# Seven products instead of eight for the last input quarter of an MLP product, and weight sums made between DRAM tensors

## The chip, the cores and the metric

The kernel runs on one core of one Trainium2 chip. The metric is the device time of one execution in microseconds, given as the median of several runs; smaller is better. A core has TensorE (PE, matrix products into the PSUM memory), VectorE (DVE), ScalarE (ACT) and GpSimd (POOL) for element-wise work, SyncE (SP), which here only issues transfers, and DMA engines that move data between DRAM and the on-chip memory. Each engine works through its own list of instructions in order and waits for the others by semaphores.

## The reference

One decoder layer on 512 tokens of width 1024, all in float32: a gated linear attention and a dilated attention, merged by gates, then an MLP, then a gated side input and a norm. The change concerns the MLP:

```
h2 = rmsnorm(x, ln2[i])
x = x + jnp.square(jax.nn.relu(h2 @ w_mlp1[i])) @ w_mlp2[i]
h3 = rmsnorm(x, ln3[i])
x = x + jax.nn.sigmoid(h3 @ w_pg[i]) * (p[i] @ w_pp[i])
return rmsnorm(x, ln_f)
```

`w_mlp1` is 1024 x 4096 and `w_mlp2` 4096 x 1024. The hidden vector of 4096 is the input of the second product; its four quarters of 1024 are summed up one after the other.

## The kernel before, in words

**Three products for one.** TensorE takes float32 operands in a rounded form (`F32R`). To keep float32 precision each operand is split into a high half `hi` (a rounded copy, made by ScalarE, line 324 for weights and 474 for activations) and a low half `lo` (the difference, made by VectorE, line 302), and a product becomes hi x hi, hi x lo and lo x hi (helpers `three`, `strassen`, `wide`; all of them issue their matmuls in `run`, line 338).

**Seven products for eight.** Most large products are cut into 2 x 2 blocks and computed with seven block products in the manner of Strassen and Winograd. The weight side needs the blocks A11, A12, A22 and the sums S1 = A21 + A22, S2 = S1 + A11, S4 = S2 + A12 and S3 = A11 + A21 (signs are absorbed elsewhere); the activation side needs B11, B21, B22 and the sums T1 to T4. For the first MLP product (`w_mlp1`) there are eight products `m1q0` to `m1q7`, each a call of `strassen` with seven stages of 24 matmuls of 256 columns. For the second (`w_mlp2`) `m2_seven` goes through the list `MLP2` of pairs (operand, quarter): each pair is one step of 24 matmuls of 512 columns, fed by two weight tiles of 128 x 1024. Before the change `SEVEN = (1, 2, 3)`: quarter 0 is computed plainly by `m2_plain(0)` and `m2_plain(1)`, two times 96 matmuls of 512 columns with eight weight tiles, ahead of `m2_seven`.

**Weights.** All weight tiles are lined up in `OPERANDS`. `weight(name)` calls `fetch`, which works ahead of TensorE: for tile i it issues the low half on VectorE, for i + 1 the high half on ScalarE, for i + 2 sums (`sums`), for i + 3 the load (`prepare`, `load`: an SP transfer of 512 KB, line 245). Here i is two tiles ahead of the one that TensorE is to use. There are eight raw buffers (`NRAW`), five for high halves and four for low halves (`NW = 5`, `NW - 1`). A sum is made in one of two ways. Either POOL issues a transfer that adds the second block onto the first while it lands (`accum_op`; line 253 for the sums listed in `EARLY`, line 281 for S3 of the 256-column products, line 319 for S4 behind the low half of S2), or VectorE adds two tiles (lines 266, 269, 275, 278, 284).

**Side work.** `run` issues matmuls in pieces, and after each piece `step` takes one closure from the list `later` and, every `pace` columns, one step from the generators in `side`. So the order of the element-wise work on each engine is fixed by hand, between the matmuls. `hid_operands` is such a generator: for each pair of `MLP2` it makes the differences T1 to T4 on VectorE (lines 1538 and 622), the high halves on ScalarE and the low halves on VectorE, two tiles of 128 x 512 each. Activations live in one pool of 68 tiles (`NU`).

**The two ends.** At the start TensorE runs `NWARM` matmuls on a tile of ones (line 566) until the first operands are there; the first product (line 594) needs `xh`, made by ScalarE from x, and `hi`, made by ScalarE from the weights (line 579). At the end the last row block of the last product (`pg1`) is cut at column `LAST = 384` into two pieces; each goes through a gate on ScalarE (line 1710), two VectorE steps (lines 1716, 1717) and a square on ScalarE (line 1721), and the root (line 1736) and the output wait for the second piece. `final` finishes a block of the second MLP product: it adds onto the residual x (line 1575, in `onto`), squares it for the norm (line 1603), and transposes it on TensorE (line 1608).

Of the kernel before, what the change touches and what calls it, by code (L numbers as in the profile page):

```python
# [19 lines left out]
P = 128  # L20
# [14 lines left out]
def att_col(g, which):  # L35
# [6 lines left out]
MLP2 = (("A11", 1), ("S1", 1), ("S2", 1), ("A11", 2), ("S1", 2), ("S4", 1), ("S2", 2), ("A11", 3), ("S1", 3), ("S4", 2),  # L42
        ("S2", 3), ("A12", 1), ("S4", 3), ("A12", 2), ("S3", 1), ("S3", 2), ("S3", 3), ("A12", 3),
        ("A22", 1), ("A22", 2), ("A22", 3))
XOF = {"A11": "B11", "S1": "T1", "S2": "T2", "S4": "B22", "A12": "B21", "S3": "T3", "A22": "T4"}
SEVEN = (1, 2, 3)


def weight_units():
# [44 lines left out]
    for sub in range(2):  # L94
        tm(f"m2p{sub}", "w_mlp2", sub * 512)
# [58 lines left out]
def early():  # L154
    after_wide = False
    for n, i in OPERAND.items():
        q, _, what = n.partition(".")
        if what == "S1":
            EARLY.setdefault(max(i - (4 if after_wide else 6), 0), []).append((n, f"{q}.A21", f"{q}.A22"))
            after_wide = False  # L160
        elif what[:3] == "S1." and q.startswith("m2c"):
# [21 lines left out]
LAST = 384  # L183
# [3 lines left out]
NWARM = 9  # L187
# [3 lines left out]
def block_kernel(ctx, tc, xT, x, ws, pT, wts, wha, wa2, vec, lnf, rel, onehot, ident_d, mask_d, out):  # L191
# [51 lines left out]
    def load(name):  # L243
        w = wst.tile([P, 1024], F32, tag="w", name="w")
        SY.dma_start(w, wts[UNIT[name]])
        return w

    def prepare(i):

        name = OPERANDS[i]  # L250
        for n, a, b in EARLY.get(i, ()):
            w = raw[n] = load(a)
            GP.dma_start(w, wts[UNIT[b]], accum_op=OP.add)  # L253
        if name in UNIT:
            raw[name] = load(name)
        elif name in S4_LOADED:
            raw[name] = load(name.replace("S4", "A12"))

    S4_LOADED = [f"m2c{SEVEN[-1]}.S4.{i}" for i in range(2)]

    def sums(i):
        q, _, what = OPERANDS[i].partition(".")
        if q.startswith("m2c"):
            if what[:3] == "S2.":
                w = raw[OPERANDS[i]] = raw[f"{q}.S1{what[2:]}"]
                V.tensor_tensor(w, w, raw[f"{q}.A11{what[2:]}"], op=OP.add)
            elif OPERANDS[i] in S4_LOADED:
                w = raw[OPERANDS[i]]
                V.tensor_tensor(w, w, raw[f"{q}.S2{what[2:]}"], op=OP.add)
        elif q == "wo" and what[:3] == "S4.":  # L270
# [35 lines left out]
    def fetch(upto):  # L306

        while done[0] < min(upto, len(OPERANDS) - 1):
            i = done[0] = done[0] + 1
            if i >= 0:  # L310
# [6 lines left out]
                if (q == "wo" or q.startswith("m2c")) and what[:3] == "S2." and f"{q}.S4{what[2:]}" not in S4_LOADED:  # L317
                    w = raw[f"{q}.S4{what[2:]}"] = raw[OPERANDS[i]]
                    GP.dma_start(w, wts[UNIT[f"{q}.A12{what[2:]}"]], accum_op=OP.add)
# [255 lines left out]
    for k in range(KC):  # L575
# [3 lines left out]
        S.activation(hi, wr[k], AF.Copy)  # L579
# [658 lines left out]
    def gates(name, i, res, make):  # L1238
# [8 lines left out]
        strassen(f"{name}{i}", xs_op, finish)  # L1247
# [35 lines left out]
    later.extend(merge(j) for j in range(KC))  # L1283
    for i in range(2):
        gates("ga", i, ga, sigmoid)
# [207 lines left out]
    hid, hb, hx = [None] * 8, {}, {}  # L1493
# [4 lines left out]
    def quad(q):  # L1498


        def finish(m, t, s, ps):
# [5 lines left out]
            def act():  # L1507
                if q // 2 in SEVEN:
                    S.activation(s, s, AF.Square)  # L1509
                    hb[q, m, t] = s  # L1510
                    return
                for n in range(2):
                    j = 4 * q + 2 * n + m
                    if hid[j] is None:
                        hid[j] = u32()
                    S.activation(hid[j][:, halves(t)], s[:, halves(n)], AF.Square)
# [3 lines left out]
        strassen(f"m1q{q}", x1_op, finish, extra=first_splits(0) if q == 7 else None)  # L1520

    hs = {}

    def hid_splits(n):
        for k in range(len(hs), len(hs) + n):
            hs[k] = split(hid[k])

    def first_splits(n):

        def extra(i):  # L1530
            if 3 <= i:
                later.append(lambda: hid_splits(1))
        return extra

    def hid_operands():
# [5 lines left out]
        for op, c in MLP2:  # L1541
            name = XOF[op]
            b11, b12, b21, b22 = ([hb[2 * c + g, k, t] for g in range(2)] for k in range(2) for t in range(2))
# [24 lines left out]
    drain()  # L1568
# [3 lines left out]
    def onto(m, t, n, ps, neg=None):  # L1572

        o, c = x2[m, t, n], 2 * t + n
        V.scalar_tensor_tensor(out=o, in0=ps, scalar=norm2[m if neg is None else neg][:, c:c + 1], in1=o, op0=OP.mult, op1=OP.add)

    def m2_plain(sub):

        ps = [mmt() if sub else smt() for _ in range(4)]
        for kk in range(4):  # L1580
            wh, wl = weight(f"m2p{sub}.{kk}")
            mms = []
            for k in range(2 * kk, 2 * kk + 2):
                xh, xl = hs[k]
                for tt in range(4):
                    c, w = slice(tt * P, (tt + 1) * P), slice((k % 2) * 512, (k % 2 + 1) * 512)
                    mms += [(ps[tt], xh[:, c], wh[:, w], k == 0, False), (ps[tt], xl[:, c], wh[:, w], False, False),
                            (ps[tt], xh[:, c], wl[:, w], False, k == 7)]
            run(mms)
            if len(hs) < 8:  # L1590
                hid_splits(2)
                if len(hs) == 8:
                    side.append(hid_operands())
        for tt in range(4):
            later.append(lambda tt=tt: onto(sub, tt // 2, tt % 2, ps[tt], 0))

    def final(m, t, n, ps, bank):
# [17 lines left out]
        later.append(go)  # L1615
        later.append(lambda: later.append(turn))
# [244 lines left out]
```

## Time and profile before

| | |
|---|---|
| median of three runs | 947.93 us (946.8 to 948.13) |
| the profiled execution | 946.6 us, its span 944.8 us |
| granted TensorE clock, mean | 0.998 |
| first MLP product, from the chain | 569.93 to 731.22 us |
| plain quarter of the second, from the chain | 731.22 to 774.78 us |
| packets of DMA | 158.75 MB, 168 GB/s over the span |

The profile shows one execution. The span is the time from the first to the last instruction; the execution's own time is a little longer. The chain is the work that ended last, followed back from the end: at each step to what released it, or to the instruction before it on its engine. Rows of it give the start, the length, the engine and the line, and how many instructions were merged. Groups give an instruction's line, engine, operation, output and inputs, shape and count, then busy time and mean ns, then the idle time of the engine ahead of it. Matmuls overlap in the pipeline, so their mean duration is longer than their spacing.

### The profile page before, as it was taken

How to read it: one execution, taken by the hardware profiler on the slowest of the kernel's cores; microseconds unless marked ns; L12 is line 12 of the kernel's file. 1: busy time of each engine (PE TensorE's matmuls, PEld its weight loads, DVE VectorE, ACT ScalarE, POOL GpSimd, SP SyncE). 2: the span in 40 equal slices, each digit the busy share in tenths (PEclk: the TensorE clock that was granted, in tenths of full speed). 3: DMA queues.
4: the chain of work that ended last, by engine and by line, in shares of the span. 5: the costliest groups of instructions: out<-in, count | busy, mean ns of one | idle time of the engine just before them, and what ended most of it. 6: DMA issues, size and time to landing. Idle time of an engine off the chain costs nothing.

```text
span 944.8 us, 15151 instructions
## 1 busy us (share of the span) xinstructions
PE 936.2 (99%) x5860; PEld 844.8 (89%) x5860; DVE 737.9 (78%) x1040; ACT 555.6 (59%) x918; POOL 113.2 (12%) x157
## 2 busy tenths in 40 slices
PE   9999999999999999999999999999999999999996
PEld 8789998899988888999988889999999888888886
DVE  7698869866789579978968779776677789897664
ACT  7357546545675578775743578665556536655543
POOL 0150010120100012022100300100000101021000
PEclk9999999999999999999999999999999999999999
DMA  9474482873817456555654788666546718599202
GB/s 356 141 234 113 133 202 68 280 237 109 189 58 212 166 134 201 135 134 179 183 148 116 177 216 256 161 172 179 157 112 166 191 49 194 148 268 368 88 1 90
DMA packets 49354, 158.75 MB, mean 168 GB/s; under 512 B 7108, under 2 KB 7696, under 8 KB 49281
## 3 DMA queue, kind: packets, MB, share of 16 engines
q1 hardware_dynamic: 31104, 103.76, 31.6%
q0 software_dynamic: 14496, 49.51, 26.5%
q10 hardware_dynamic: 3680, 4.51, 1.3%
q8 instruction: 46, 0.75, 0.3%
q14 instruction: 28, 0.22, 0.1%
HBM read 149.32 MB, written 10.26 MB: 169 GB/s over the span
## 4 chain that ended last, share of the span: by engine, by line
PE 96%; issue 1%; DVE 1%; DMA 1%; ACT 0%; POOL 0%; POOLq 0%; DVEq 0%; ACTq 0%
PE mmt L338 75%; PE smt L338 12%; PE mmt L594 2%; PE smt L1028 2%; DMA u<-y_dram 1%; PE smt L968 1%; PE smt L891 1%; PE smt L566 0%; PE smt L861 0%; PE smt L985 0%; PE smt L984 0%; PE smt L860 0%; PE smt L974 0%; PE smt L1412 0%; PE smt L1084 0%
## 5 line engine op out<-in xcount | busy, mean ns | idle before, releaser
L338 PE MATMUL mmt<-ur,hi 128*128 128x256 f32 (+1 forms) x2192 | 436.4, 297 | 0.0
L338 PEld LDWEIGHTS mmt<-ur,hi 128*128 128x128 f32 x2192 | 349.7, 189 | 11.8
L302 DVE TENSOR_TENSOR lo<-w,hi 128x1024 fp32r<-128x1024 f32 x254 | 308.6, 1219 | 60.5 <-PE mmt L338 37.0
L338 PE MATMUL mmt<-ur,lo 128*128 128x256 f32 (+1 forms) x1096 | 326.6, 298 | 0.5 <-DVE lo L302 0.5
L324 ACT ACTIVATE hi<-w 128x1024 fp32r<-128x1024 f32 x254 | 265.4, 1055 | 101.9 <-PE mmt L338 24.8
L338 PE MATMUL mmt<-hi,ur 128*128 128x512 f32 (+3 forms) x912 | 266.2, 375 | 0.0
L338 PEld LDWEIGHTS mmt<-ur,lo 128*128 128x128 f32 x1096 | 206.6, 189 | 6.3 <-DVE lo L302 0.7
L338 PEld LDWEIGHTS mmt<-hi,ur 128*128 128x128 f32 x912 | 165.3, 188 | 28.6
L338 PE MATMUL mmt<-lo,ur 128*128 128x512 f32 (+3 forms) x456 | 170.6, 374 | 0.0
L474 ACT ACTIVATE ur<-u 128x512 fp32r<-128x512 f32 x113 | 67.5, 625 | 65.3 <-DVE u L622 17.1
L338 PEld LDWEIGHTS mmt<-lo,ur 128*128 128x128 f32 x456 | 85.7, 188 | 15.1
L338 PE MATMUL smt<-hi,ur 128*128 128x512 f32 x288 | 89.1, 390 | 0.0
L302 DVE TENSOR_TENSOR ur<-u,ur 128x512 fp32r<-128x512 f32 x112 | 73.6, 685 | 10.8 <-ACT ur L474 10.2
L467 DVE TENSOR_TENSOR u<-u,mmt 128x512 f32<-128x512 f32 (+1 forms) x94 | 58.0, 648 | 27.2 <-PE mmt L338 26.9
L253 POOL DMA_DIRECT2D w<-in_wts_dram x46 | 43.5, 993 | 249.8 <-DMA w<-in_wts_dram 145.3
L408 ACT ACTIVATE u<-mmt 128x512 f32<-128x512 f32 x72 | 42.9, 596 | 51.0 <-PE mmt L338 50.8
L338 PEld LDWEIGHTS smt<-hi,ur 128*128 128x128 f32 x288 | 53.8, 188 | 10.9
L338 PE MATMUL smt<-lo,ur 128*128 128x512 f32 x144 | 56.0, 389 | 0.0
L281 POOL DMA_DIRECT2D w<-in_wts_dram x18 | 16.1, 894 | 282.0 <-DVE w L278 158.1
L338 PEld LDWEIGHTS smt<-lo,ur 128*128 128x128 f32 x144 | 27.0, 188 | 5.7
L1509 ACT ACTIVATE u<-u 128x512 f32<-128x512 f32 x24 | 15.0, 628 | 26.7 <-DVE u L1505 26.7
L844 ACT ACTIVATE u<-u,st 128x256 f32<-128x256 f32 (+1 forms) x32 | 15.6, 488 | 12.5 <-DVE st L840 11.0
(242 smaller groups left out, 848.0 us busy)
## 6 DMA issues: line engine op xcount, KB each, us to landing
w<-in_wts_dram SPq DMA_DIRECT2D x182, 512.0 KB, 5.1
w<-in_wts_dram POOLq DMA_DIRECT2D x70, 512.0 KB, 7.1
u<-in_xT_dram SPq DMA_DIRECT2D x8, 256.0 KB, 5.2
u<-in_ws_dram SPq DMA_DIRECT2D x8, 256.0 KB, 5.3
v_dram<-u ACTq DMA_DIRECT2D x8, 256.0 KB, 6.4
u<-v_dram POOLq DMA_DIRECT2D x8, 256.0 KB, 6.5
y_dram<-u ACTq DMA_DIRECT2D x8, 256.0 KB, 2.2
u<-y_dram POOLq DMA_DIRECT2D x8, 256.0 KB, 7.0
```

The lines of the kernel that those rows point to most:

```text
L253: GP.dma_start(w, wts[UNIT[b]], accum_op=OP.add)
L281: GP.dma_start(w, wts[UNIT[f"{q}.A21"]], accum_op=OP.add)
L302: V.tensor_tensor(lo, x, hi.bitcast(F32), op=OP.subtract)
L324: S.activation(hi[:, s], w[:, s], AF.Copy, scale=1.0 if c is None else c)
L338: TE.matmul(o, lhsT=l, rhs=r, start=a, stop=b, skip_group_check=shared)
L408: S.activation(sums[c], bank[b], AF.Copy, scale=-scale if c[0] else scale)
L467: V.tensor_tensor(out, s, ps, op=OP.subtract if m else OP.add)
L474: S.activation(hi, x, AF.Copy)
L594: TE.matmul(q0ps[i], lhsT=(hi, hi, lo)[j][:, c], rhs=(xh, xl, xh)[j], start=not k and not j, stop=k == KC - 1 and j == 2)
L844: S.activation(q3[:, a, s:], q3[:, a, s:], AF.Exp, bias=nm[:, col + a:col + a + 1], accum_out=sums[:, col + a:col + a + 1])
L1028: TE.matmul(o, lhsT=l[a][:, lc], rhs=r[b], start=start and i == 0, stop=stop and i == 2)
L1509: S.activation(s, s, AF.Square)
```

## The change

All four quarters of the second product go through `m2_seven`, in a new order of the list `MLP2`; `m2_plain` is gone, and so is the `drain()` between the two MLP products. VectorE adds no sums of `w_mlp2` any more (before: S2 of each quarter and S4 of the last): once the low half of S1 is made, POOL adds A11 onto the same raw tile for S2, and behind the low half of S2 it adds A12 for S4. S1 of all quarters and S3 of quarters 0 and 1 (`STORED`, six sums of two tiles each) are made in DRAM ahead of time: SP copies the first block into a DRAM tile, POOL adds the second one onto it, and later SP loads the sum as it would load a weight. The generator `stores` issues these a step at a time, at two of the seven stages of the gates `ga`, after each of the eight `og` products, and at two stages of `m1q0` to `m1q6`. The hidden operands of the first six pairs are made during the last five stages of `m1q7`; the rest when the second product has begun.

At the start there is one warm-up matmul less, and the first weight high half is copied by VectorE. At the end the last row block is cut 256 + 256. Three of the four transposes of `final` get one empty step ahead of them.

```diff
-SEVEN = (1, 2, 3)
+SEVEN = (0, 1, 2, 3)
+STORED = tuple(("S1", c) for c in SEVEN) + (("S3", 0), ("S3", 1))
...
+MLP2 = (("A11", 0), ("S1", 0), ("A11", 1), ("A11", 2), ("S2", 0), ("S1", 1), ("A11", 3), ("S4", 0), ("S2", 1), ("S1", 2),
+        ("A12", 0), ("S4", 1), ("S2", 2), ("S1", 3), ("A12", 1), ("S4", 2), ("S2", 3), ("A12", 2), ("S3", 0), ("S4", 3),
+        ("S3", 1), ("S3", 2), ("S3", 3), ("A12", 3), ("A22", 0), ("A22", 1), ("A22", 2), ("A22", 3))
...
-LAST = 384
+LAST = 256
...
-NWARM = 9
+NWARM = 8
...
-        SY.dma_start(w, wts[UNIT[name]])
+        SY.dma_start(w, stored[name] if name in stored else wts[UNIT[name]])
...
+    def store(name):
+
+        q, _, what = name.partition(".")
+        a, b = ("A21", "A22") if what[1] == "1" else ("A11", "A21")
+        t = stored[name] = dr.tile([P, 1024], F32, name=name.replace(".", "_"))
+        SY.dma_start(t, wts[UNIT[f"{q}.{a}{what[2:]}"]])
+
+        def accumulate():
+            GP.dma_start(t, wts[UNIT[f"{q}.{b}{what[2:]}"]], accum_op=OP.add, max_dma_last_dim=1024)
+        return accumulate
+
+    def stores():
+
+        names = [f"m2c{c}.{op}.{i}" for op, c in STORED for i in range(2)]
+        todo = [store(name) for name in names[:2]]
+        yield
+        for name in names[2:]:
+            todo.append(store(name))
+            yield
+            todo.pop(0)()
+            yield
+        for f in todo:
+            f()
+            yield
...
-        if q.startswith("m2c"):
-            if what[:3] == "S2.":
-                w = raw[OPERANDS[i]] = raw[f"{q}.S1{what[2:]}"]
-                V.tensor_tensor(w, w, raw[f"{q}.A11{what[2:]}"], op=OP.add)
...
+        if q.startswith("m2c") or (q == "wo" and what[:3] == "S4."):
             return
...
+                for a, b, c in (("S1", "S2", "A11"), ("S2", "S4", "A12")):
+                    if what[:3] == a + "." and (q.startswith("m2c") or (q == "wo" and a == "S2")):
+                        w = raw[f"{q}.{b}{what[2:]}"] = raw[OPERANDS[i]]
+                        GP.dma_start(w, wts[UNIT[f"{q}.{c}{what[2:]}"]], accum_op=OP.add)
...
-        S.activation(hi, wr[k], AF.Copy)
+        if k:
+            S.activation(hi, wr[k], AF.Copy)
+        else:
+            V.tensor_copy(hi, wr[k])
...
+            if q < 7 and i % 3 == 2:
+                next(spare, None)
+            if q == 7 and i == 1:
+                side.append(hid_operands())
...
+            while len(hx) >= 6 and not second:
+                yield
...
-    drain()
...
+        if (m, t) != (1, 0):
+            later.append(rest)
...
-    m2_plain(0)
-    m2_plain(1)
+    second.append(True)
     m2_seven()
```

More of the change, by code (lines that the diff above doesn't have):

```diff
@@ L160, in early @@
             after_wide = False
+        elif q.startswith("m2c") and (what[:2], int(q[3:])) in STORED:
+            continue
         elif what[:3] == "S1." and q.startswith("m2c"):
@@ L1490, in block_kernel @@
     side.append(stats())
-    hid, hb, hx = [None] * 8, {}, {}
+    hb, hx, second = {}, {}, []
     def x1_op(name, pr):
@@ L1567, in block_kernel, with onto @@
         quad(q)
-    drain()
     lnb, rt3 = [], []
     x3, ss3 = {}, const.tile([P, 8], F32, name="ss3")
-    def onto(m, t, n, ps, neg=None):
+    def onto(m, t, n, ps):
         o, c = x2[m, t, n], 2 * t + n
[L1575 to L1595, printed above, removed]
+        V.scalar_tensor_tensor(out=o, in0=ps, scalar=norm2[m][:, c:c + 1], in1=o, op0=OP.mult, op1=OP.add)
     def final(m, t, n, ps, bank):
```

49 lines of the change are left out of this document (13 added, 36 removed).

## The prediction

> **What bounds the kernel now.** I read the page first, then the chain that ended last, then the stages from the first MLP product to the end of the second in the windows view, and last the groups, the waits and the DMA views.
>
> ```profile
> span 944.8 us, 15151 instructions
> PE 936.2 (99%) x5860; PEld 844.8 (89%) x5860; DVE 737.9 (78%) x1040; ACT 555.6 (59%) x918; POOL 113.2 (12%) x157
> ...
> PE 96%; issue 1%; DVE 1%; DMA 1%; ACT 0%; POOL 0%; POOLq 0%; DVEq 0%; ACTq 0%
> ```
>
> TensorE is the bound nearly everywhere: 96% of the chain. What counts is therefore the number of matmuls times their spacing, and whether anybody makes TensorE wait. The chain gives the spacing, since its pieces run from one release to the next (the mean of one matmul in the groups holds pipeline depth and is longer):
>
> ```profile
> 1.00 4.21 PE smt L566 x18
> ...
> 569.93 161.29 PE mmt L338 x1344
> 731.22 21.80 PE smt L338 x96
> ...
> 774.78 10.88 PE smt L338 x48
> ...
> 840.06 5.44 PE mmt L338 x24
> ```
>
> The first product is 1344 matmuls of 256 columns in 161.29 us: 0.120 us each, 2.88 us for a stage of 24. The plain quarter of the second is 192 of 512 columns, 731.22 to 774.78: 43.56 us, or 0.2269 each. An operand step of the seven-product part is 24 in 5.44 us (0.2267 each), so one weight tile (12 matmuls) lasts 2.72 us. No piece of another engine stands between: TensorE doesn't wait in these stages.
>
> Beside it VectorE is nearly full:
>
> ```profile
> 690.90:711.00 20.10, 20.10 (x169) 20.10 (x169) 14.70 (x18) 11.40 (x16) 0.87 (x1) 1.00 0.47 131
> 711.00:731.20 20.20, 20.20 (x170) 20.20 (x169) 14.10 (x19) 13.25 (x19) 0.87 (x1) 1.00 0.73 178
> 731.20:774.80 43.60, 43.60 (x194) 36.09 (x193) 34.01 (x46) 20.41 (x30) 2.62 (x3) 1.00 0.50 133
> 774.80:829.20 54.40, 54.40 (x241) 45.06 (x241) 49.81 (x59) 33.82 (x45) 7.08 (x8) 1.00 0.67 158
> 829.20:851.00 21.80, 21.80 (x97) 18.03 (x97) 21.80 (x29) 11.71 (x14) 5.68 (x9) 1.00 1.01 287
> ```
>
> The columns are the window, its length, then PE, PEld, DVE, ACT, POOL, the granted clock (1.00) and DMA share. VectorE is busy in all 21.80 us from 829.20 on and TensorE loses nothing there: it lives on weights prepared ahead. How far ahead, the waits of the first product and the code tell:
>
> ```profile
> DVE lo L302 <- PE mmt L338: 23.3, 19, 1.7
> ```
>
> VectorE waits 19 times for TensorE before a low half: the four low buffers are full. A low half then starts when TensorE leaves the tile four back and ends three tiles less its own duration before it is used. With the first row below that is 3 x 2.88 - 1.22 = 7.4 us ahead in the first product and 3 x 2.72 - 1.22 = 6.9 us in the second. This lead is what a delay may eat.
>
> ```profile
> L302 DVE TENSOR_TENSOR lo<-w,hi 128x1024 fp32r<-128x1024 f32 x48 | 58.4, 1221 | 12.8 <-PE mmt L338 4.7 <-ACT hi L324 3.2 <-issue 3.0
> L302 DVE TENSOR_TENSOR ur<-u,ur 128x512 fp32r<-128x512 f32 x47 | 30.3, 685 | 1.8 <-ACT ur L474 1.7
> L1538 DVE TENSOR_TENSOR u<-u 128x512 f32<-128x512 f32 x12 | 7.7, 684 | 0.0
> L266 DVE TENSOR_TENSOR w<-w 128x1024 f32<-128x1024 f32 x6 | 7.3, 1221 | 0.1
> ...
> L1575 DVE SCALAR_TENSOR_TENSOR u<-u,n 128x512 f32<-128x512 f32 x4 | 2.8, 746 | 0.0
> ```
>
> **The change, part by part.** The profiled execution took 946.6 us, 1.8 outside its span, and lies 1.3 below the median of 947.93; I make the sum against it and carry the difference over to the median.
>
> **Matmuls.** The fourth quarter becomes 7 x 24 = 168 matmuls instead of 192: 24 x 0.2267 = **-5.44 us**, all on the path, as PE bounds the stage on both sides.
>
> **VectorE over the whole stage.** Removed: the eight weight sums (8 x 1.22 = 9.8), the plain quarter's eight low halves (9.8), eight splits (8 x 0.685 = 5.5) and eight additions onto the residual (8 x 0.75 = 6.0): 31.1. Added: 14 low halves (17.1), 14 splits (9.6), eight differences (5.5): 32.2. The three windows from 731.20 to 851.00 hold 34.01 + 49.81 + 21.80 = 105.6 us of work in 119.8; with +1.1 work and 5.4 less time it is 93%, and 82% once the 12.3 us of the next paragraph lie ahead of the stage: it fits, at zero cost. ScalarE gets six more high halves and six more splits, at the rows below 6 x 1.06 + 6 x 0.63 = 10 us on an engine that is busy 33.82 of 54.40: zero as well.
>
> ```profile
> L324 ACT ACTIVATE hi<-w 128x1024 fp32r<-128x1024 f32 x254 | 265.4, 1055 | 101.9 <-PE mmt L338 24.8 <-DVE w L284 14.5 <-issue 11.4
> ...
> L474 ACT ACTIVATE ur<-u 128x512 fp32r<-128x512 f32 x113 | 67.5, 625 | 65.3 <-DVE u L622 17.1 <-DVE u L613 12.5 <-DVE u L528 11.2
> ```
>
> **The hand-over.** Here the cover is thin. The plain quarter gave 43.6 us of light work in which the hidden operands were made. Now six operands are made in the last five stages (14.4 us) of the last product of MLP 1, and queue on VectorE ahead of the low halves: 12 splits and 6 differences of 0.685, 12.3 us. A product like the one from 690.90 leaves VectorE 20.1 - 14.7 = 5.4 us idle, five sevenths of it 3.9. VectorE is thus 8.4 us behind when MLP 1 ends, against a lead of 7.4: TensorE waits 1.0 us. The next steps need 2 x 1.22 and a split pair or two in 5.44 us, so the lag then shrinks. Overlap of neighbouring instructions makes the lag smaller, ScalarE's turn in each split larger. Bounds: 0 (lag below the lead) and 3.4 (lag 10% larger, and a step of the split chain lost); I take the worked value, **+1.0**. The drain() that goes costs nothing by itself: it only moves the last squares behind the first weights, and the quarter they feed starts six steps later (32 us).
>
> **Weight sums on the second stage.** S2 and S4 now come from accumulating DMAs into the same tile: the accumulation is issued after S1's low half, and S2's high half is made five tiles later, 5 x 2.72 = 13.6 us.
>
> ```profile
> w<-in_wts_dram SPq DMA_DIRECT2D x182, 512.0 KB, 5.1
> w<-in_wts_dram POOLq DMA_DIRECT2D x70, 512.0 KB, 7.1
> ...
> cb_dram<-c_dram POOLq DMA_DIRECT2D x4, 448.0 KB, 6.7
> ```
>
> At 7.1 us it lands 6.5 before it is needed, and the lead comes on top: zero; past 13.6 + 6.9 = 20.5 us each further microsecond would be TensorE's. There are 20 accumulations into SBUF in the stage instead of 16, and 40 loads as before.
>
> **Stored sums.** The list holds six sums of two tiles: 12 copies on SP and 12 accumulations on POOL, from the gates to the sixth product of MLP 1. No row shows an accumulation in DRAM. Its DMA time from below is that of one into SBUF, from above twice that:
>
> ```profile
> q1 hardware_dynamic: 31104, 103.76, 31.6%
> q0 software_dynamic: 14496, 49.51, 26.5%
> ```
>
> 31.6% of 944.8 us for 103.76 MB is 347 GB/s, so a copy of 0.524 MB takes 1.5 us of all engines (3.0 if writing counts fully); 26.5% for 49.51 MB is 198 GB/s, 2.65 us (5.3). Twelve pairs are 50 us (to 100). They lie in over 190 us (192 and 168 matmuls of 0.227 ahead of 569.93, five and a half products of 20.2 behind it), mostly where the share looks like this:
>
> ```profile
> 590.00:600.00 10.00, 10.00 (x85) 10.00 (x85) 8.37 (x13) 9.39 (x20) 0.87 (x1) 1.00 0.98 233
> 600.00:610.00 10.00, 10.00 (x86) 10.00 (x85) 6.64 (x9) 4.38 (x9) 1.40 (x2) 1.00 0.27 90
> ```
>
> A mean of 0.62 goes to about 0.9; at the upper end the DMA engines are full there. On SP each copy stands ahead of later weight loads and delays them by 1.5 to 3 us; on POOL each accumulation waits for its copy (issued two steps before) and then costs about 0.7 us of issue (113.2 / 157), ahead of the accumulations for MLP 1's S1 and S3. Such an S3 has four stages, 11.5 us, less 7.1: 4.4 us, and the lead of 7.4 behind that. I take zero, bounds 0 and +2.
>
> **Start.** One warm-up matmul less is two of 18 passes: 2 x 4.21 / 18 = 0.47. The first real matmul also needs the first high half, now copied on VectorE:
>
> ```profile
> 1.19 0.42 SPq L554 DMA_DIRECT2D u<-in_ws_dram  x1
> ...
> 4.39 0.61 ACT L579 ACTIVATE ur<-u 128x512 fp32r<-128x512 f32 x1
> 4.52 0.75 DVE L304 SCALAR_TENSOR_TENSOR ur<-u,cv,ur 128x512 fp32r<-128x512 f32 x1 [3.65 <-ACT ur L476]
> ```
>
> ```profile
> DMA to landing us min/median/max: 3.1/5.3/6.1
> ```
>
> The weights land at 1.19 + 3.1 = 4.3; a copy of 0.4 to 0.6 on the idle VectorE ends at 4.7 to 4.9 instead of 5.0. That is **-0.3** (0 to -0.47); VectorE's next work at 4.52 moves back as much, and its result is needed only four matmuls later.
>
> **End.** The last row block is cut 256 + 256 instead of 384 + 128.
>
> ```profile
> 930.83 0.34 PE L338 MATMUL mmt<-lo,ur 128*128 128x384 f32 x1
> ...
> 934.50 0.33 PE L338 MATMUL mmt<-lo,ur 128*128 128x384 f32 x1
> ...
> 934.91 0.27 PE L338 MATMUL mmt<-lo,ur 128*128 128x128 f32 x1
> ...
> 937.25 0.28 PE L338 MATMUL mmt<-lo,ur 128*128 128x128 f32 x1
> ```
>
> Each pair of rows spans 21 matmuls: 0.175 us at 384 columns, 0.111 at 128. Now 24 x 0.286 = 6.86; with 48 of 256 at 0.120, 5.76: -1.1. Behind the last matmul stand one gate, two VectorE steps and a square on the second piece:
>
> ```profile
> 935.29 0.56 ACT L1710 ACTIVATE u<-mmt,rt 128x384 f32<-128x384 f32 x1
> ...
> 937.68 0.37 ACT L1710 ACTIVATE u<-mmt,rt 128x128 f32<-128x128 f32 x1 [1.82 <-PE mmt L338]
> ```
>
> ```profile
> 935.88 0.56 DVE L1716 TENSOR_TENSOR u<-u 128x384 f32<-128x384 f32 x1 [0.47 <-ACT u L1710]
> ...
> 938.08 0.29 DVE L1716 TENSOR_TENSOR u<-u 128x128 f32<-128x128 f32 x1 [1.04 <-ACT u L1710]
> ```
>
> Halfway between the two widths each grows by 0.1 to 0.13, four times: +0.45. Net **-0.65** (0 to -0.8). The Trainium skill, "TensorE: Matmul & The Clock Gate", section "Back-to-back issue gap", gives N / 2.4 + 2.5 ns: 162 and 56 ns where the rows have 175 and 111. By that both cuts take 5.24 us and the edit would lose 0.45. The rows don't bear it out at 128 columns; the page's section on LDWEIGHTS (128 / 1.2 = 107 ns) fits the 111 better.
>
> The empty steps put ahead of three transposes cost nothing: TensorE's work fills them. **Sum:** -5.44 + 1.0 - 0.3 - 0.65 = -5.4: 941.2 beside the profiled 946.6, **942.5** beside the median.
>
> **The rivals.** (1) No wait at the hand-over: for it that VectorE's rows overlap a little; 941.5. (2) VectorE becomes the bound across it: the splits go ScalarE, VectorE by turns, each waiting for the other, and the freed tiles come only as TensorE finishes stages, so 3 to 6 us are lost instead of 1.0; 944.5 to 947.5, 945.5 as its middle. For it: the full window at 829.20; against it: that window cost TensorE nothing. (3) Slower: the accumulation in DRAM is slow and holds POOL's queue, so S3 of MLP 1 comes late. Seven accumulations fall in MLP 1; each costs what it delays beyond 4.4 + 7.4 = 11.8 us. From 12.6 us of delay apiece the gain is used up (7 x 0.8), at 15 it is 22 us, 965. Against it: 6.7 us for 448 KB between DRAM tensors, and idle DMA stretches of 0.27. (4) The spacing goes with the columns alone (0.227 for 512 however they are cut, 5.44 us for both cuts), so the last cut gains nothing and its longer tail stands: 942.5 + 0.65 + 0.45 = 943.6. The spacing of 0.111 at 128 columns speaks against it. The skill's formula named above is this rival.
>
> **How the numbers follow.** 0.2% is 1.9 us, about what a measurement here can tell from no change. Forecast 0.61, (1) 0.12, (2) 0.17, (3) 0.07, (4) 0.03. Faster by more: all of the forecast, (1) and (4), and 0.11 of (2): 0.87. Within: 0.06, of (2). Slower: 0.07. The range runs from start and end at their best without a wait (947.93 - 5.44 - 0.47 - 0.8 = 941.2, less 0.4 for the median's own scatter, 946.8 to 948.13 before) to just past the middle of (2), which also takes in the +2 of the stored sums: 945.8.
>
> **What would show it.** A chain of TensorE from the first product to the end of the second, that of the second some 152.3 us for 672 matmuls; one wait of TensorE for a low half near the seam and none later; VectorE full there, around 82% after; the first real matmul near 4.8; the end pieces 2.88 us each. Wrong would be: waits for low halves on through the second product, ScalarE waiting for accumulated tiles in MLP 1, or accumulations in DRAM that take over 12 us.

## The result, and the profile after

The changed kernel takes 941.43 us (median of 6 executions, 939.97 to 942.85) beside 947.47 for the kernel before (median of 6, 946.8 to 948.13): a ratio of 0.9935, 95% interval 0.9925 to 0.9945. The profiled execution took 939.98 us with a span of 938.2, against 946.6 and 944.8.

The page of the changed kernel: the span, the busy time of each engine, and the shares of the chain that ended last.

```profile
span 938.2 us, 15155 instructions
...
PE 929.3 (99%) x5834; PEld 838.3 (89%) x5834; DVE 739.1 (79%) x1045; ACT 563.8 (60%) x921; POOL 130.2 (14%) x173
...
PE 95%; DMA 2%; DVE 1%; ACT 1%; issue 1%; POOL 0%; POOLq 0%; DVEq 0%; SPq 0%; ACTq 0%
```

TensorE has 26 records fewer (24 matmuls and two passes of the warm-up), and is still the bound. In the last line the DMA has grown from 1% of the chain to 2%. The chain itself, in order of time (start, length, what):

```profile
42.38 34.57 PE mmt L357 x160
...
529.16 12.61 DMA w<-in_wts_dram
...
549.96 5.49 PE mmt L357 x24
...
569.94 161.29 PE mmt L357 x1344
731.23 21.80 PE smt L357 x96
...
893.63 31.77 PE mmt L357 x140
925.43 0.70 ACT u L1707
```

and the corresponding ends of the same chain in the kernel before:

```profile
42.79 34.57 PE mmt L338 x160
...
899.06 31.77 PE mmt L338 x140
930.86 0.70 ACT u L1710
```

MLP 1 begins at 569.94 (before: 569.93) and takes 161.29 us as before. From its start to the end of the piece of 140 matmuls it is 925.40 - 569.94 = 355.46 us, against 930.83 - 569.93 = 360.90: the **5.44 us** of 24 matmuls. TensorE waits nowhere between, not at the hand-over either: the 96 matmuls from 731.23 on take 21.80 us as 96 others did before. The rest of the 6.6 us lies behind 925.4: 938.2 - 925.40 = 12.80 against 944.8 - 930.83 = 13.97.

The stages of the second product show VectorE a little less full than before in the middle and at the end (columns as in the prediction):

```profile
731.20:774.80 43.60, 43.60 (x194) 36.08 (x193) 36.65 (x46) 28.34 (x39) 7.64 (x9) 1.00 0.82 187
774.80:829.20 54.40, 54.40 (x241) 45.05 (x241) 45.26 (x56) 31.98 (x41) 8.14 (x10) 1.00 0.90 212
829.20:851.00 21.80, 21.80 (x101) 18.07 (x101) 20.67 (x28) 14.66 (x22) 7.18 (x12) 1.00 0.98 309
```

36.65 + 45.26 + 20.67 = 102.6 us in 119.8, 86%. The accumulations of the stored sums in the list of DMA issues (count, KB, median us to landing):

```profile
m2c_S<-in_wts_dram POOLq DMA_DIRECT2D x12, 512.0 KB, 10.8
```

An accumulation within DRAM lands after 10.8 us in the median, against 7.1 for one into the on-chip memory (SBUF) before. Some take longer: the one issued at 459.07 lands after 14.5 us, and the longest transfer of these tiles takes 18.0. The prediction named over 12 us as a sign of being wrong; it came, and TensorE lost nothing by it: MLP 1 takes 161.29 us, and the stored sums are loaded from 698 on only.

One thing in the chain wasn't foreseen. In this execution TensorE is 0.41 us earlier at 42, and by the gated output it is 1.15 earlier (chain pieces at 468.84 and 469.99; the profile of before had lost 0.5 of that to its wait for a low half in the `ga` gates). All of it is gone at 569.9. The waits name the place:

```profile
PE smt L1436 <- DVE u L486: 0.8, 2, 0.5
```

In the output projection an accumulating DMA (POOL, issued at 529.16) lands 12.61 us later (11.5 in the profile of before), the high and low halves made from its tile follow, the addition L486 stands behind them on VectorE, and TensorE's transposes wait for it.

### The profile page after: what moved, and what is told of

Read it like the earlier page. It is cut to its first block, busy times and chain, and to the rows that moved or that the text cites. A ratio compares the mean times of both kernels' runs of the same rounds, so it can differ in the third digit from the quotient of the medians.

```text
span 938.2 us, 15155 instructions
## 1 busy us (share of the span) xinstructions
PE 929.3 (99%) x5834; PEld 838.3 (89%) x5834; DVE 739.1 (79%) x1045; ACT 563.8 (60%) x921; POOL 130.2 (14%) x173
## 4 chain that ended last, share of the span: by engine, by line
PE 95%; DMA 2%; DVE 1%; ACT 1%; issue 1%; POOL 0%; POOLq 0%; DVEq 0%; SPq 0%; ACTq 0%
PE mmt L357 74%; PE smt L357 11%; PE mmt L616 2%; PE smt L1050 2%; DMA w<-in_wts_dram 1%; PE smt L990 1%; PE smt L913 1%; PE smt L883 0%; PE smt L1007 0%; PE smt L1006 0%; PE smt L882 0%; PE smt L996 0%; PE smt L1206 0%; PE smt L1106 0%; DMA u<-in_ws_dram 0%
## 5 line engine op out<-in xcount | busy, mean ns | idle before, releaser
L320 DVE TENSOR_TENSOR lo<-w,hi 128x1024 fp32r<-128x1024 f32 x260 | 316.1, 1221 | 59.7 <-PE mmt L357 33.5
L343 ACT ACTIVATE hi<-w 128x1024 fp32r<-128x1024 f32 x260 | 271.9, 1055 | 90.2 <-PE mmt L357 17.5
L357 PE MATMUL mmt<-hi,ur 128*128 128x512 f32 (+1 forms) x912 | 265.4, 375 | 0.0
L357 PE MATMUL mmt<-lo,ur 128*128 128x512 f32 (+1 forms) x456 | 170.2, 373 | 0.0
L493 ACT ACTIVATE ur<-u 128x512 fp32r<-128x512 f32 x119 | 70.8, 626 | 62.9 <-DVE u L644 14.9
L320 DVE TENSOR_TENSOR ur<-u,ur 128x512 fp32r<-128x512 f32 x118 | 77.4, 687 | 11.3 <-ACT ur L493 10.7
L357 PE MATMUL smt<-hi,ur 128*128 128x512 f32 x272 | 84.1, 390 | 0.0
L486 DVE TENSOR_TENSOR u<-u,mmt 128x512 f32<-128x512 f32 (+1 forms) x94 | 58.0, 651 | 26.7 <-PE mmt L357 26.5
L255 POOL DMA_DIRECT2D w<-in_wts_dram x38 | 38.3, 1062 | 184.6 <-DMA w<-in_wts_dram 81.5
L299 POOL DMA_DIRECT2D w<-in_wts_dram x18 | 16.2, 898 | 273.5 <-DVE w L296 132.7
L357 PE MATMUL smt<-lo,ur 128*128 128x512 f32 x136 | 52.9, 389 | 0.0
L1532 ACT ACTIVATE u<-u 128x512 f32<-128x512 f32 x32 | 20.1, 628 | 31.0 <-DVE u L1529 30.9
L338 POOL DMA_DIRECT2D w<-in_wts_dram x18 | 16.6, 920 | 120.5 <-DVE lo L320 60.5
## 6 DMA issues: line engine op xcount, KB each, us to landing
m2c_S<-in_wts_dram POOLq DMA_DIRECT2D x12, 512.0 KB, 10.8
```

What stands on the lines that cost most here:

```text
L299: GP.dma_start(w, wts[UNIT[f"{q}.A21"]], accum_op=OP.add)
L320: V.tensor_tensor(lo, x, hi.bitcast(F32), op=OP.subtract)
L338: GP.dma_start(w, wts[UNIT[f"{q}.{c}{what[2:]}"]], accum_op=OP.add)
L343: S.activation(hi[:, s], w[:, s], AF.Copy, scale=1.0 if c is None else c)
L357: TE.matmul(o, lhsT=l, rhs=r, start=a, stop=b, skip_group_check=shared)
L486: V.tensor_tensor(out, s, ps, op=OP.subtract if m else OP.add)
```

## The experiments

My theory was that the gain is the 24 matmuls and the balance of the last cut, and that the start's gain is swallowed by the burst of transfers in the output projection. The rivals were that the start counts, that the stored sums' traffic costs or saves something, and that the hand-over is free for another reason than VectorE's lead. Each ratio below is against the kernel before, run on the same chip beside it.

The whole time scatters by 1 to 3 us, more than most of these effects. So I cut each profile at three events of the chain that all kernels have: the start of the piece of 160 matmuls near 42, the start of MLP 1, and the end of the piece of 140. Both chains above show them.

| kernel | first stretch, to the 160 | to MLP 1 | MLP 1 to the 140's end | tail to the span's end | ratio, 95% interval |
|---|---|---|---|---|---|
| before | 42.79 | 527.14 | 360.90 | 13.97 | |
| before, second profile (b_again) | 42.59 | 526.56 | 360.90 | 13.95 | |
| before + ends (b_ends) | 42.39 | 528.18 | 360.90 | 13.43 | 0.9985, 0.9976 to 0.9993 |
| before + residual loads (b_x4) | 43.06 | 526.81 | 360.90 | 14.03 | 0.9994, 0.9985 to 1.0003 |
| changed | 42.38 | 527.56 | 355.46 | 12.80 | 0.9935, 0.9925 to 0.9945 |
| old start (a_start) | 42.66 | 530.63 | 355.46 | 12.85 | 0.9952, 0.9939 to 0.9964 |
| old end (a_end) | 42.62 | 528.27 | 355.46 | 13.35 | 0.9951, 0.9938 to 0.9965 |
| no stored sums (a_none) | 42.67 | 528.20 | 355.46 | 13.07 | 0.9933, 0.9921 to 0.9945 |
| 8 extra differences (a_seam8) | 42.38 | 528.42 | 355.46 | 12.84 | 0.9931, 0.9917 to 0.9945 |
| 16 extra differences (a_seam16) | 42.89 | 527.92 | 362.60 | 12.79 | 1.0026, 1.0016 to 1.0036 |
| no operands ahead (a_cold) | 43.18 | 527.46 | 361.27 | 12.79 | 1.0016, 1.0007 to 1.0025 |
| residual loads, four (a_x4) | 43.03 | 526.83 | 355.45 | 12.79 | 0.9918, 0.9902 to 0.9935 |
| residual loads, six, none stored (n_x6) | 42.75 | 526.88 | 355.46 | 13.01 | 0.9920, 0.9906 to 0.9934 |

The third stretch is 360.90 in every kernel with the plain quarter, and 355.46 to 0.01 us in every one with seven products in which TensorE waits neither in MLP 1 nor at the hand-over. The second varies by 4 us, in kernels that hold nearly the same instructions there.

**The start undone.**

```
-        if k:
-            S.activation(hi, wr[k], AF.Copy)
-        else:
-            V.tensor_copy(hi, wr[k])
+        S.activation(hi, wr[k], AF.Copy)
...
-NWARM = 8
+NWARM = 9
```

> The changed kernel with its start put back (nine warm-up products, first high half on ScalarE). Theory: the start's gain never reaches the end. The trace of the changed kernel is 0.41 us ahead at the first product of the `ga` gates and 1.13 ahead at the `og` stage, yet MLP 1 begins at 569.94 against 569.93 before, because the output projection waits for accumulations that land at 541.77 in both traces. Then this kernel equals the changed one within 0.3 us (about 941.4), its first real matmul is at 5.1 instead of 4.9, and MLP 1 begins at 570 again. Rival: the start counts in full and the arrival at 569.9 is chance; then it is 0.4 us slower than the changed kernel (941.8).

Both were wrong in size: this execution is slower by more than either, and not for its start. At 42 it is 42.66, 0.28 behind the changed kernel; but MLP 1 begins at 573.29. Its chain and windows:

```profile
529.42 14.11 DMA w<-in_wts_dram
...
552.46 6.34 PE mmt L357 x24
```

```profile
552.00:556.00 4.00, 4.00 (x16) 3.28 (x15) 3.03 (x5) 3.92 (x7) 0.00 (x0) 0.73 1.07 222
```

The same accumulation took 14.11 us instead of 12.61, TensorE's wait for L486 was 2.2 us, and the 24 matmuls behind it took 6.34 instead of 5.49, at a granted clock of 0.73. What the start itself is worth, the first column says: the ten profiles with the new start reach the piece of 160 at 42.38 to 43.18, in the mean 42.74 (the run with late stored sums is the tenth, 43.09); the four with the old one at 42.59 to 43.06, in the mean 42.78. No gain is seen; single profiles with the same start differ by 0.8, so one as small as 0.3 isn't excluded either.

**The end undone.**

```
-LAST = 256
+LAST = 384
```

> The changed kernel with its end put back (last row block cut 384 + 128). Theory: the finer balance of the last cut is worth what the two traces show between the last whole row's gate and the last step, 9.17 against 8.59 us, so this kernel is 0.6 us slower than the changed one (942.0), with 24 matmuls of 384 columns in 4.2 us and 24 of 128 in 2.7. Rival: the spacing goes with the columns alone, the last cut gains nothing and its longer tail is a loss; then this kernel is 0.4 us faster (941.0).

The tail is 13.35 instead of 12.80: 0.55 us for the cut, as the theory had it, and the rival's gain is refuted. The whole time agrees in sign but is too coarse: its ratio's interval overlaps the changed kernel's.

**The two ends alone, on the kernel before.**

```
-LAST = 384
+LAST = 256
...
-NWARM = 9
+NWARM = 8
...
-        S.activation(hi, wr[k], AF.Copy)
+        if k:
+            S.activation(hi, wr[k], AF.Copy)
+        else:
+            V.tensor_copy(hi, wr[k])
```

> The kernel before with only the two ends of the change (eight warm-up products, first high half on VectorE, last cut 256). Theory: only the end counts, 0.6 us faster than before (946.9 beside a median of 947.5), and the start's 0.2 to 0.4 us is lost by 570. Rival: both count, 1.0 faster (946.5). If the whole change but these ends is worth the 24 matmuls, the distance from this kernel to the changed one is 5.4 us.

The ratio of 0.9985 is 1.4 us (0.7 to 2.3), more than the theory's 0.6; the rival's 1.0 lies inside, so the whole time doesn't decide what the start is worth. The tail gives 0.54. Its profiled execution shows the wait for L467 (the same addition) with 1.4 us, without a single stored sum in the kernel. So the stored sums aren't needed for that wait. The tail shows one thing more: 13.43 here and 12.80 in the changed kernel with the same cut. 0.6 us came with the change and not with the cut. In the kernel before and in the run with the old end, which share the cut, it lies behind the last step on VectorE:

```profile
930.86 0.70 ACT u L1710
...
940.03 0.48 DVE u L1744
```

```profile
926.38 0.70 ACT u L1707
...
935.55 0.48 DVE u L1741
```

From gate to last step it is 9.17 in both; from there to the span's end 944.8 - 940.51 = 4.29 and 939.7 - 936.03 = 3.67. The views show nothing there that differs but its length. Part of it goes with the stored sums: the two kernels without them have tails of 13.07 and 13.01 in the table, the others with the change and its cut 12.79 to 12.85. So some 0.25 of the 0.6 us came with the stored sums, by a way that stays open.

**All stored sums during MLP 1.**

```
-        strassen(f"{name}{i}", xs_op, finish, extra=lambda i: i % 3 == 2 and name == "ga" and next(spare, None))
+        strassen(f"{name}{i}", xs_op, finish)
...
-        next(spare, None)
...
-            if q < 7 and i % 3 == 2:
+            if q < 7 and i % 2 == 0:
```

> The changed kernel with all stored weight sums made during MLP 1 (four steps of the generator in each of its first seven products) and none during the `ga` gates and the gated output. Theory: the output projection's wait of about 1.1 us comes from its own burst of transfers (DMA share 1.02 to 1.08 from 530 to 550), which the stored sums don't touch since none runs between 510 and 565: the wait stays and the time is that of the changed kernel within 0.4 us (941.4). Rival: their traffic ahead of the burst pushes it; then the wait of TensorE for L486 goes, MLP 1 begins about 1 us earlier, and the time is 940.4. Third possibility: 24 transfers in seven products of MLP 1 crowd its own S1 and S3 sums, TensorE waits there, and it is slower by over 1 us.

The third possibility: ratio 0.9989 (0.9980 to 0.9998), 5 us slower than the changed kernel. The waits, the chain, the transfers and the clock:

```profile
PE mmt L357 <- ACT u L427: 6.0, 1, 6.0
```

```profile
591.70 19.93 DMA w<-in_wts_dram
```

```profile
m2c_S<-in_wts_dram POOLq DMA_DIRECT2D x12, 512.0 KB, 19.2
```

```profile
610.00:620.00 10.00, 5.27 (x24) 5.27 (x25) 6.90 (x9) 5.50 (x8) 0.57 (x1) 0.53 1.01 205
```

The accumulation at 591.70 is for an S3 of MLP 1. POOL issues it behind one in DRAM (at 588.95), it lands after 19.93 us, ScalarE waits for it before a high half, TensorE waits 6.0 us for ScalarE, and the clock behind that is 0.53. The forecast's rival (3) is a real mechanism. Its arithmetic gives 19.9 - 11.8 = 8.1 us, and from the piece near 42 to the end of the 140 this kernel takes 891.28 us (43.09 to 934.37), 8.3 more than the changed one (883.02); but that they agree is partly luck, since the wait itself is 6.0, and the rest lies in the slower clock and a longer wait in the output projection. The wait in the output projection stayed (1.3 us at L486) with no stored sum ahead of it, as the theory said.

**No stored sums.**

```
-STORED = tuple(("S1", c) for c in SEVEN) + (("S3", 0), ("S3", 1))
+STORED = ()
...
```

> The changed kernel with no stored sums: S1 and S3 of every quarter are accumulated into SBUF tiles ahead of their use, as S1 and S3 of the kernel before were. It adds 12 accumulations into SBUF to the second product (32 instead of 20) and takes 24 transfers out of the stages ahead. Theory: at 2.65 us of all DMA engines each (50 MB at 198 GB/s) the 12 extra accumulations need 32 us of a stage of 152 whose DMA share is 0.8 to 0.9, less 12 loads of 1.5; the DMA queues fill up in 775 to 880, accumulations land later than their three tiles (8.2 us) plus the lead of 7, and TensorE waits in the second product for 5 to 20 us in all. Rival: the DMA engines keep up, and the stored sums buy nothing; then the time is that of the changed kernel within 0.5 us, or up to 1 us better if the stored sums' traffic was what lost the gain at the output projection.

The theory fell. The third stretch is 355.46, the ratio 0.9933. The stage is full in this run, and nothing waits for it:

```profile
774.80:829.20 54.40, 54.40 (x242) 45.05 (x241) 45.09 (x56) 32.00 (x40) 13.14 (x15) 1.00 1.04 247
```

The share of 1.04 in the last column but one is that of the DMA engines. Accumulations from the weights into SBUF land after 7.3 us in the median of this run (6.6 in the changed kernel); each has its tiles' time and VectorE's lead, and no wait of TensorE for a weight shows. The twelve stored tiles buy nothing that the whole time or the stretches show.

**No operand made ahead.**

```
-            if q == 7 and i == 1:
-                side.append(hid_operands())
...
+    while side or later:
+        step()
     second.append(True)
+    side.append(hid_operands())
+    while len(hx) < 6:
+        step()
     m2_seven()
```

> The changed kernel with no hidden operand made during the last product of MLP 1: that product's squares are finished first, then the first six operands are made, then the second product begins (what comes later is as it was). Theory: the operands made ahead are the hand-over's cover. Without them TensorE waits for the first operand (the last addition 1.3, the squares 1.3, high halves 1.3 and low halves 1.2 in turn, some 4 to 5 us) and for low halves queued behind the six operands' 11 us of VectorE work, less the lead of 7: 5 to 8 us slower in all (947 to 949). Rival: VectorE's lead covers this too, and the wait is under 2 us (943).

The third stretch is 361.27, 5.81 us longer, within the theory's 5 to 8.

```profile
PE smt L357 <- ACT ur L493: 3.4, 1, 3.4
```

```profile
735.32 0.70 DVE ur L320
...
736.06 23.46 PE smt L357 x95
```

MLP 1's last matmul ends at 731.94, TensorE starts again at 736.06, 4.1 us later, and the next 95 matmuls take 23.46 instead of some 21.5. The first part of the theory, the wait for the first operand, is there. The second, low halves late behind the operands, is not: no wait for one shows, and the loss behind the seam goes with a granted clock of 0.50:

```profile
737.15:740.56 3.41, 3.41 (x10) 2.67 (x9) 3.31 (x7) 3.31 (x6) 0.00 (x0) 0.50 0.00 0
```

The operands made ahead are the cover; without them the second product gives back all that it won.

**Extra work at the seam, eight and sixteen differences.**

```
+    busy = u32()
+    for _ in range(8):
+        V.tensor_tensor(busy, hb[0, 0, 0], hb[0, 1, 0], op=OP.subtract)
     second.append(True)
```

> The changed kernel with eight extra VectorE differences (0.6 to 0.69 us each, 4.8 to 5.5 in all, result unused) queued between the last product of MLP 1 and the second product. Theory: the hand-over leaves VectorE's low halves 4 to 6 us ahead of TensorE, since the six operands lie between low halves of tiles two stages on and not in front of them; this load fits or costs at most 0.5 us (941.4 to 942). The forecast's arithmetic (VectorE 8.4 us behind against a lead of 7.4) would make it cost all of 5 us (946.5).

> As the one before with sixteen extra differences (9.6 to 11 us). Theory: what goes beyond the lead of 5 to 6 is TensorE's wait: 4 to 5.5 us slower (945.5 to 947), one wait for a low half just behind the seam. The forecast's arithmetic makes it 10 to 11 us slower (952). Rival: VectorE's idle stretches behind the seam (1.55 at 747) take it all up, under 2 us.

Eight cost nothing (355.46); sixteen cost 362.60 - 355.46 = 7.1 us. VectorE's timeline with eight:

```profile
730.35 5.77 DVE L1685 TENSOR_TENSOR u<-u 128x512 f32<-128x512 f32 x8
736.03 1.22 DVE L320 TENSOR_TENSOR lo<-w,hi 128x1024 fp32r<-128x1024 f32 x1
```

and with sixteen, the same queue, then the wait, the chain and the clock:

```profile
730.37 11.58 DVE L1685 TENSOR_TENSOR u<-u 128x512 f32<-128x512 f32 x16
```

```profile
PE smt L357 <- DVE lo L320: 5.1, 1, 5.1
```

```profile
741.86 1.23 DVE lo L320
...
743.13 17.90 PE smt L357 x70
```

```profile
744.00:748.00 4.00, 4.00 (x13) 3.11 (x13) 4.00 (x7) 3.05 (x4) 1.27 (x2) 0.64 0.77 112
```

Eight hold the next low half back by 736.03 - 730.35 = 5.7 us, sixteen by 741.86 - 730.37 = 11.5; for 5.1 of these TensorE waits, so 6.4 us were spare. The other 2.0 us lie behind the wait, at a lower granted clock: 70 matmuls in 17.90 instead of 15.9. The theory had the wait and not the clock; the forecast's arithmetic falls with both runs.

**Residual tiles loaded plainly ahead**, on the changed kernel, on the kernel without stored sums (all six) and on the kernel before; and the kernel before once more.

```
-        o = sums[m, t, n] = x2[m, t, n] = u32()
+        if (m, t) == (0, 0) or (m, t) == (1, 1):
+            o = sums[m, t, n] = x2[m, t, n]
+            V.tensor_tensor(o, o, ps, op=OP.subtract if m else OP.add)
+            return
+        o = sums[m, t, n] = x2[m, t, n] = u32()
         S.activation(o, ps, AF.Copy, scale=-1.0 if m else 1.0)
...
-    for n in range(2):
-        x2[1, 0, n] = u32()
-        GP.dma_start(x2[1, 0, n], x_rows(1, 0, n))
+    for m, t in ((1, 0), (0, 0), (1, 1),):
+        for n in range(2):
+            x2[m, t, n] = u32()
+            GP.dma_start(x2[m, t, n], x_rows(m, t, n))
```

> The changed kernel with four of the six residual tiles that the output projection accumulates by DMA (u<-in_x, 256 KB each) loaded plainly ahead of it instead, where the DMA share is 0.05 (508 to 520), and added by VectorE (0.69 us each). Theory: the start's gain is lost because the accumulation issued at about 529.2 lands 12.6 to 14.1 us later, behind two of these and in a burst with the others; with them gone it lands 2 to 3 us earlier, TensorE doesn't wait for L486, MLP 1 begins at 568.8 to 569.2 instead of 569.9 to 573.3, and the time is 1.0 to 2.0 us below the changed kernel (939.4 to 940.4), with less scatter. Rival: the burst's length is set by the weights' own sums, or VectorE's four additions come late and hold the banks: no gain (within 0.4), or a loss up to 1 us.

> No stored sums, and all six residual tiles loaded plainly ahead of the output projection. Theory: stored sums buy nothing and the six tiles are the burst: as the run with four or up to 0.5 us better (939 to 940.4). Rival: without the accumulations of the last two tiles nothing more is won, and VectorE's 4 us of additions in a stage where it is busy 60 to 80% cost TensorE a wait: 0.5 us slower than the run with four.

> The kernel before with four residual tiles loaded plainly ahead, nothing else. Theory: the output projection's wait for its accumulation is in the kernel before too, in most executions (its profiled one happens to lose 0.2 us there): 0.5 to 1.2 us faster than before (946.3 to 947 beside 947.5). Rival: it is the change that brought the wait; then no difference (within 0.3).

> The kernel before once more, for a second profile. Theory: its 0.5 us wait at the `ga` gates (for a transfer of y that took 6.8 us) and the landing of the output projection's accumulation differ from one execution to the next; MLP 1 begins between 569.5 and 572. Rival: they are fixed, and MLP 1 begins at 569.9 again with the same waits.

The wait for L486 is gone in all three kernels with these loads, and the second stretch is 526.83, 526.88 and 526.81: where it varied by 4 us it now agrees to 0.07. In the run with four, the accumulation of the weights that stood behind the residual tiles is issued at 531.25 and lands after 5.3 us, at 536.6, instead of after 12.61, at 541.77: 5 us earlier, where the theory had 2 to 3. The chain of the run with four and its only wait of TensorE behind the start:

```profile
527.14 0.61 DVE u L1403
...
527.88 5.73 PE mmt L357 x24
```

```profile
PE mmt L357 <- DVE u L1403: 0.2, 1, 0.2
```

What is left is 0.2 us for VectorE's addition, the small form of the rival. With 939.64 us (939.35 to 940.31) and 939.91 (939.50 to 940.08) these two are the fastest kernels of the study; the intervals of their ratios (0.9902 to 0.9935, 0.9906 to 0.9934) still touch the changed kernel's, and the trace is the better witness. MLP 1's arrival at 569.86 in the first is not earlier than the changed kernel's 569.94 only because its first stretch happened to be 0.65 longer.

For the kernel before, the ratio of 0.9994 (0.9985 to 1.0003) shows no gain by these loads, but its interval holds the theory's 0.5 us as well as the rival's nothing. Its second profile has neither the 0.5 us wait at the `ga` gates nor one here: 526.56, with MLP 1 at 569.15, so these waits do differ between executions. Yet with the two ends alone the wait was there. That the landing of this accumulation differs between executions is shown (11.5 and 11.6 us in the two profiles of before, 12.55 to 14.11 in the nine others that kept it). Whether the change makes the longer ones more frequent, or where a program's buffers happen to lie in DRAM does, wasn't separated and stays open.

## Why the prediction was right, and where its terms were off

The forecast of 942.5 held in sign and size (941.43 was measured), and its main step is shown: fewer matmuls at the spacing of the chain. The other terms were off by up to 1 us each. That the sum of -5.4 came within 0.6 us of the -6.0 between the medians is partly luck: a loss that didn't come, a gain that wasn't found, and 0.6 us at the end that nobody had foreseen.

**Matmuls, -5.44.** Measured -5.44 in the third stretch, alike to 0.01 in all seven profiles with the seven products in which TensorE waits neither in MLP 1 nor at the hand-over. The spacing read from the chain (0.2267) was all that was needed.

**The hand-over, +1.0.** This is the step that failed: the term is 0, as in rival (1). The prediction, like the description of the change, counts six operands made ahead. But the generator stops like this:

```
            while len(hx) >= 6 and not second:
                yield
...
            for g in range(2):
                hx[name, c, g] = split_lo(src[g], his[g])
```

`hx` holds tiles, two for each pair of `MLP2` (one for each `g`), so it stops after three pairs. VectorE's timeline of the changed kernel shows where it really went:

```profile
718.01 1.29 DVE L320 TENSOR_TENSOR ur<-u,ur 128x512 fp32r<-128x512 f32 x2 [1.42 <-ACT ur L493]
719.22 1.29 DVE L1551 TENSOR_TENSOR u<-u 128x512 f32<-128x512 f32 x2
720.43 1.22 DVE L320 TENSOR_TENSOR lo<-w,hi 128x1024 fp32r<-128x1024 f32 x1
721.57 1.28 DVE L320 TENSOR_TENSOR ur<-u,ur 128x512 fp32r<-128x512 f32 x2
722.77 1.22 DVE L320 TENSOR_TENSOR lo<-w,hi 128x1024 fp32r<-128x1024 f32 x1
723.90 1.29 DVE L320 TENSOR_TENSOR ur<-u,ur 128x512 fp32r<-128x512 f32 x2
...
729.50 1.22 DVE L320 TENSOR_TENSOR lo<-w,hi 128x1024 fp32r<-128x1024 f32 x1
...
734.27 1.29 DVE L320 TENSOR_TENSOR ur<-u,ur 128x512 fp32r<-128x512 f32 x2
735.48 1.22 DVE L320 TENSOR_TENSOR lo<-w,hi 128x1024 fp32r<-128x1024 f32 x1
```

Ahead of the seam at 731.2 there are three pairs of splits (`ur<-u,ur`) and one of differences (L1551), 4 x 1.2 = 4.8 us in all, not 12.3; the work of the next three pairs begins at 734.27, once the second product is being issued. With three pairs the forecast's own arithmetic gives 8 x 0.685 = 5.5 us, less 3.9 idle: VectorE 1.6 us behind against a lead of 7.4, and no wait. Nor does the work stand in one piece ahead of the low halves: it alternates with them, two operations at a time, and TensorE needs a low half only every 2.72 to 2.88 us. Start to start two such operations take 1.20 us, not 2 x 0.685. The low half at 729.50 ends at 730.72, and TensorE takes it two weight tiles into the second product, at about 731.23 + 5.44 = 736.7, plus two matmuls: some 6.4 us of lead, where the forecast had -1.0. The run with sixteen differences measures the same 6.4. VectorE was nearly full from 718 to 746; being full wasn't being late. How long a hand-over with six pairs made ahead would take, no run shows.

**VectorE over the stage, S2 and S4 by DMA, all at zero.** Right: 86% busy, between the 93% with no operand work ahead of the stage and the 82% with all of six pairs ahead, and no wait for a weight in the second product.

**Stored sums, zero (0 to +2).** Right in sum, since a kernel without them takes the same time. The risk named in rival (3) is real when they are crowded into MLP 1; one case shows it, at a delay of 19.9 us, which doesn't tell from where on it costs time.

**Start, -0.3.** Not found, and too small to be excluded: the first real matmul did start earlier (4.92 against 5.06), but the end of the first stretch doesn't follow it from one execution to the next. See the last section.

**End, -0.65.** 0.55 by the cut. The page "TensorE: Matmul & The Clock Gate" of the Trainium skill, section "Back-to-back issue gap", gives a formula for the gap of an isolated matmul by which, as an estimate, this edit would have been a loss of 0.45; the measurement decides against it for these two shapes.

**Not foreseen.** 0.6 us between the last recorded step and the span's end, whose cause is open; and the wait in the output projection, with which the second stretch came out up to 4.1 us longer (530.63) than without it (526.56), and through which anything gained earlier has to pass.

## What to carry to other kernels

Count work ahead in the unit that the code's condition counts in, here tiles and not pairs, and check the count in an engine's timeline. A queue of extra work delays the bound engine only by what stands in front of each thing that it needs: follow the interleaving on the engine, step by step, against the rate at which the results are needed, before you add the whole work up. Compare kernels by stretches between events that all of them have: here the stretch that the change is about repeats to 0.01 us where the whole time scatters by 2. A gain made ahead of a stage that waits for a late transfer is not yet a gain; and a traffic saving in a stage with lead to spare buys nothing.

## What the runs showed of the hardware

The longer waits of TensorE cost more than their length. The wait of 1.6 us at L486 with eight extra differences was followed by 24 matmuls in 5.49 us; the one of 2.2 us, in two parts, by 6.34; the waits of 3.4 and 5.1 us at the hand-over by 95 and 70 matmuls that took 1.9 and 2.0 us longer than at 0.2267 each. With the last three, the granted clock is 0.50 for 3.4, 3.41 and 6.83 us. The row of the second stands in its experiment; those of the other two:

```profile
550.80:554.20 3.40, 3.40 (x12) 3.01 (x13) 2.74 (x3) 2.52 (x6) 0.87 (x1) 0.50 1.07 248
```

```profile
740.04:746.87 6.83, 3.73 (x9) 2.96 (x10) 6.76 (x11) 2.19 (x4) 1.67 (x2) 0.50 0.27 28
```

The Trainium skill, page "TensorE: Matmul & The Clock Gate", section "Part 1: The HAM clock gate", has the clock halved after an idle window of about 3.4 us that runs freely. The halving is as the trace has it; but here waits of 2.2 us were enough once, and where between 1.6 and 2.2 it begins, or whether that differs from one time to the next, no run shows.

The start scatters too. The 96 matmuls of the first product, from the chains of the changed kernel and of the run with no operands ahead:

```profile
4.92 22.04 PE mmt L616 x96
```

```profile
4.82 22.93 PE mmt L616 x96
```

The one that starts 0.1 earlier takes 0.9 longer: its first matmuls come 0.43 us apart until 6.7, the other's 0.23 from the third on. That looks like the slower clock, but the granted clock reads 1.00 there in both traces, so the cause isn't shown. That page says that the moment of warming up differs between runs. Whatever the cause, a warm-up matmul more or less can't be judged from one profile.
